# Raw gate banks, earlier squares and paired chains at the four joints of a hybrid encoder layer

## The chip, the cores and the metric

The kernel runs on one core of one Trainium2 chip. The metric is the device time of one execution in microseconds, the median of three runs. TensorE is PE in the profile, VectorE DVE, ScalarE ACT, GpSimd POOL; SyncE (SP) issues the DMAs.

## The reference

One layer over 1024 tokens of width 1024, all in float32. Every sub-layer has its own norm, and the two SwiGLUs enter with a factor of one half:

```
def rmsnorm(x, g):
    return x * lax.rsqrt(jnp.mean(x * x, axis=-1, keepdims=True) + EPS) * g

def swiglu(h, w_gu, w_down):
    gate, up = jnp.split(h @ w_gu, 2, axis=-1)
    return (jax.nn.silu(gate) * up) @ w_down

x = x + 0.5 * swiglu(rmsnorm(x, ffn1_norm), ffn1_w_gu, ffn1_w_down)
h = rmsnorm(x, mix_norm); proj = h @ w_in        # HGRN2 group, stick-breaking group (q, k, v)
x = x + concat(hgrn2(...), stick_breaking(...)) @ w_out
x = x + memory_cross_attention(rmsnorm(x, mem_q_norm), rmsnorm(mem, mem_kv_norm), ...)
x = x + 0.5 * swiglu(rmsnorm(x, ffn2_norm), ffn2_w_gu, ffn2_w_down)
return rmsnorm(x, final_norm)
```

Widths: 1024 (model), 2816 (SwiGLU), 256 memory tokens in 4 heads, 8 stick-breaking heads of 64.

## The kernel before

Activations lie transposed: 8 chunks of 128 channels (c) by two halves of 512 tokens (hf). An fp32 product is made of three fp32r matmuls (`mm3`): high by high, low by high, high by low part. A chain of 8 such steps, 24 matmuls of 512 columns, fills one PSUM bank. The high part of a factor is an ACT copy, the low part a DVE subtraction (`factor`, `split`, `lift_chunk`).

The norm is applied after the matmul: with h = x·g as factor, a projection is multiplied by 1/rms of its token. For that, squares of the chunks (ACT) are summed over chunks (POOL, `arrive`), summed over partitions by one-column matmuls against `ones` (`sums_of_squares`), turned into 1/rms by twelve small DVE operations (`rsqrt`), and spread over 128 partitions by four 128x128 matmuls against `ident`, which ACT copies to the tile `rs` (`spread`).

A SwiGLU works on products of 512x512 blocks in a Strassen-Winograd scheme: seven products (A11, S1, S2, A12, S3, S4, A22) of sums of activations (tiles T1 to T4, made by `sums_12`, `sums_3`, `sums_4` on POOL, ACT and DVE) and sums of weights (`r` from HBM, `S` on POOL, `f` high on ACT and low on DVE). `pairs` weaves two such jobs; `pairs.start(n)` issues the weight work of the first products ahead, `pairs.run` the rest, `pairs.defer(n, step)` puts a step behind the n-th product. Ahead of the products stand plain chains for the first 256 columns: gates (banks X, Y), ups (Z, Z, X, Y). In the first SwiGLU the gate banks are still in PSUM when 1/rms comes. `between` scales them with `rs` (DVE), applies Silu (ACT), multiplies by `rs` again (POOL), so that `s` = silu(gate) × 1/rms, and the ups are multiplied in.

In the second SwiGLU (`stored=True`) the gates were made inside cross-attention (`gate_steps`), copied to HBM (`gd`) and loaded back. Its `rs` needs the last chunk that cross-attention delivers. The last two gate chains run one after the other, with the sums for the second token half between them.

At the end of the first SwiGLU the last chunks arrive, `inv_rms_both` (in `to_mixers`) makes the mixers' 1/rms, and `sb_proj(0, r)` runs chains for q and k of both halves in the two `acc` banks, with `spread_both` before step 7, then the values. Scores (`z_steps`, bank z) and their products of 1 - sigmoid (tile `om`: ACT, POOL mask, DVE scan) follow.

Engines run their queues in order. A planner (Tile) orders what the program issues by priority and dependences, and `tc.issue_after` pins an instruction behind another.

## Time and profile before

| | us |
|---|---|
| median of 3 runs | 2268.94 |
| lowest, highest run | 2266.56, 2270.53 |
| profiled execution | 2266.65 |
| its span | 2264.9 |
| PE busy in the span | 2192.8 |
| DVE, ACT, POOL busy | 1661.7, 1003.8, 730.4 |
| mean granted clock of PE | 0.993 |

The span is from the first to the last instruction of the profiled execution; that execution's own time has 1.75 us around it. PE is busy for 97% of the span, but "busy" counts a matmul at half clock as well as one at full clock. The idle rest is 72.1 us. The list of PE's waits names the larger pieces of it, and windows of the span give the granted clock of each stretch.

### The profile page before, as it was taken

The page shows a single profiled execution, that of the slowest core. Times are in us where ns is not written, and L with a number is a line of the kernel's source. Part 1 is how long each engine was busy: PE and PEld are TensorE (multiplying, and loading weights), DVE is VectorE, ACT ScalarE, POOL GpSimd, SP SyncE. Part 2 cuts the span into 40 slices and gives each one's busy share as a digit, 9 for nine tenths or more (in the row PEclk, how much of TensorE's full clock was granted, in tenths as well). Part 3 has the DMA queues.
Part 4 walks back from the last instruction along what each step waited for, and adds up shares of the span by engine and source line. Part 5 has one row for each costly group of instructions (what it writes and reads, how often), then busy time and mean ns, then how long its engine had stood idle before and what let it go on. Part 6 is the DMA issues. An engine that isn't in the chain of part 4 may idle for free.

```text
span 2264.9 us, 30630 instructions
## 1 busy us (share of the span) xinstructions
PE 2192.8 (97%) x10952; PEld 1837.0 (81%) x10952; DVE 1661.7 (73%) x2732; ACT 1003.8 (44%) x1905; POOL 730.4 (32%) x700
## 2 busy tenths in 40 slices
PE   8999999999999999999989999999999999999997
PEld 6888888878778787888879888887778888887876
DVE  7877777768986869778787455667786767685896
ACT  7544434443355536454464243224543444444334
POOL 3563535334541102020131020001355343443553
PEclk9999999999999999999999999999999999999999
DMA  8334434766721001100115311111342333377552
GB/s 298 130 128 135 142 128 147 254 213 215 244 96 38 23 25 29 38 29 19 38 54 161 93 48 47 47 38 47 125 145 93 131 120 126 124 259 233 180 175 75
DMA packets 220568, 265.75 MB, mean 117 GB/s; under 512 B 13440, under 2 KB 144512, under 8 KB 220416
## 3 DMA queue, kind: packets, MB, share of 16 engines
q1 hardware_dynamic: 220416, 263.80, 35.5%
q8 instruction: 86, 1.41, 0.3%
q14 instruction: 66, 0.54, 0.1%
HBM read 187.47 MB, written 76.28 MB: 116 GB/s over the span
## 4 chain that ended last, share of the span: by engine, by line
PE 79%; DVE 12%; ACT 3%; issue 2%; DMA 2%; POOL 1%; SPq 0%; POOLq 0%; DVEq 0%; ACTq 0%
PE X L82 26%; PE Y L82 13%; PE Z L82 6%; PE acc L127 4%; PE acc L129 4%; PE acc L128 4%; PE q L128 2%; PE q L127 2%; PE q L129 2%; DVE E L82 1%; DVE om L1143 1%; PE wo L129 1%; PE wo L127 1%; PE wo L128 1%; PE dn L127 1%
## 5 line engine op out<-in xcount | busy, mean ns | idle before, releaser
L82 PE MATMUL X<-T,f 128*128 128x512 f32 x1464 | 345.2, 391 | 3.7 <-ACT e L82 3.3
L82 PEld LDWEIGHTS X<-T,f 128*128 128x128 f32 x1464 | 275.4, 188 | 62.4 <-ACT e L82 3.8
L82 PE MATMUL X<-hh,f 128*128 128x512 f32 x975 | 311.9, 390 | 1.3 <-DVE E L82 0.9
L82 ACT ACTIVATE f<-S 128x512 fp32r<-128x512 f32 (+2 forms) x256 | 155.6, 609 | 269.6 <-POOL S L82 256.4
L82 DVE TENSOR_TENSOR f<-S,f 128x512 fp32r<-128x512 f32 (+2 forms) x256 | 226.3, 896 | 26.1 <-ACT f L82 25.4
L82 PEld LDWEIGHTS X<-hh,f 128*128 128x128 f32 x975 | 183.0, 188 | 41.9 <-issue 2.4
L82 POOL TENSOR_TENSOR E<-E,rs 128x512 f32<-128x512 f32 x104 | 170.4, 1638 | 126.4 <-DVE E L82 109.1
L82 DVE TENSOR_TENSOR f<-r,f 128x512 fp32r<-128x512 f32 (+2 forms) x192 | 201.3, 1065 | 0.0
L82 PE MATMUL X<-hl,f 128*128 128x512 f32 x488 | 190.9, 391 | 3.6 <-DVE hl L82 3.6
L82 POOL TENSOR_TENSOR S<-r,r 128x512 f32<-128x512 f32 (+2 forms) x64 | 94.1, 1470 | 307.9 <-DMA r<-in_ffn_w_down_dram 93.9
L82 PE MATMUL Y<-T,f 128*128 128x512 f32 x732 | 176.4, 389 | 0.0
L82 PE MATMUL Y<-hh,f 128*128 128x512 f32 x488 | 160.7, 389 | 0.0
L82 PEld LDWEIGHTS Y<-T,f 128*128 128x128 f32 x732 | 137.4, 188 | 28.7
L82 PE MATMUL Z<-hh,f 128*128 128x512 f32 x488 | 160.6, 389 | 0.0
L127 PE MATMUL acc<-hh,wh 128*128 128x512 f32 (+1 forms) x384 | 151.6, 395 | 0.0
L128 PE MATMUL acc<-hl,wh 128*128 128x512 f32 (+1 forms) x384 | 145.6, 379 | 2.5 <-DMA hl<-msl 2.5
L129 PE MATMUL acc<-hh,wl 128*128 128x512 f32 (+1 forms) x384 | 146.5, 382 | 0.0
L82 DVE TENSOR_TENSOR E<-X,E 128x512 f32<-128x512 f32 x100 | 68.7, 687 | 101.6 <-PE X L82 100.9
L82 POOL TENSOR_TENSOR S<-S,r 128x512 f32<-128x512 f32 (+2 forms) x64 | 83.2, 1300 | 180.7 <-DVE f L82 146.5
L1140 POOL TENSOR_SCALAR_AFFINE_SELECT om<-om 128x128 f32<-128x128 f32 x64 | 27.2, 425 | 340.3 <-ACT om L1135 340.0
L82 ACT ACTIVATE E<-X 128x512 f32<-128x512 f32 x102 | 60.5, 593 | 165.2 <-PE X L82 165.2
L107 ACT ACTIVATE wh<-wraw 128x512 fp32r<-128x512 f32 (+1 forms) x128 | 79.2, 654 | 90.5 <-PE acc L128 29.3
(455 smaller groups left out, 5433.7 us busy)
## 6 DMA issues: line engine op xcount, KB each, us to landing
r<-in_ffn_w_gu_dram SPq DMA_DIRECT2D x86, 512.0 KB, 3.8
r<-in_ffn_w_down_dram SPq DMA_DIRECT2D x32, 512.0 KB, 4.5
wraw<-in_w_in_dram SPq DMA_DIRECT2D x20, 512.0 KB, 3.6
wraw<-in_mem_w_kv_dram SPq DMA_DIRECT2D x16, 512.0 KB, 3.6
x<-in_x_cols_dram SPq DMA_DIRECT2D x16, 256.0 KB, 5.4
T<-in_x_dram SPq DMA_DIRECT2D x8, 512.0 KB, 6.1
fx<-x SPq DMA_DIRECT2D x16, 256.0 KB, 5.2
sg<-fx SPq DMA_DIRECT2D x16, 256.0 KB, 4.1
```

Of the source, the lines that this page charges most:

```text
L82: done = getattr(self.eng, name)(*args, **kw)
L107: nc.scalar.activation(hi[:, part], src[:, part], AF.Copy)
L127: nc.tensor.matmul(ps, lh, rh, start=start, stop=False)
L128: nc.tensor.matmul(ps, lh, rl, start=False, stop=False)
L129: last_mm[0] = nc.tensor.matmul(ps, ll, rh, start=False, stop=stop).ins
L1140: nc.gpsimd.affine_select(out=a[:, dg], in_=a[:, dg], compare_op=ALU.is_gt, fill=fill, base=0, pattern=[[-sign, P]], channel_multiplier=sign)
L1143: nc.vector.tensor_tensor_scan(run, run, run, 1.0 if carry is None else carry, op0=ALU.mult, op1=ALU.bypass)
```

## The change

It works at four places.

**First SwiGLU, start.** The four gate banks are copied raw to SBUF by DVE ahead of `rsqrt`; the spread of each half moves from the second Z chain into the X chain of the second half's ups and to its end; scaling follows there, from SBUF. `sums_4` of chunks 2 and 3 goes behind the first product, ahead of `sums_3`; the weight work of products 1 and 2 goes ahead of the scaling.

**First SwiGLU, end.** Squares of the first half are kept in tiles of their own (`rs0`, with chunk 7's apart in `rs1`); those of chunk 6, second half, are added by POOL. The two q chains of pair 0 stop after six of eight steps, the sums of squares stand between them and the rest, and the k chains use the z banks. The scaling of q comes after the fourth k step.

**Cross-attention.** The last head's softmax weights are scaled by ACT. The first half's sums are made when chunk 1 of the second half arrives, spread at chunk 3, and both first-half gates are finished there: DVE multiplies, ACT Silu, POOL multiplies. The last two gate chains alternate step by step in banks q and pt.

**Second SwiGLU, start.** Only the second half's gates are scaled there, after `pairs.start` of products 1 and 2; one spread stands before the second Z chain.

```diff
-    def arrive(c, hf, g0, sqp, acc, lift=True, apart=False):
+    def arrive(c, hf, g0, sqp, acc, lift=True, apart=False, kept=False):
         first = hf not in acc
-        sq = (accp if hf else sqp).tile([P, H], F32, name="sqa") if first else sqp.tile([P, H], F32, name="sq", bufs=2)
+        if kept and (first or apart):
+            sq = accp.tile([P, H], F32, name="sqa") if first and hf else rsp.tile([P, H], F32, name="rs1" if apart else "rs0")
+        else:
+            sq = (accp if hf else sqp).tile([P, H], F32, name="sqa") if first else sqp.tile([P, H], F32, name="sq", bufs=2)
...
+            def spread_one(hf):
+                with tc.issue_after(last_mm[0]):
+                    rs[hf] = spread(ys[hf], psn, "nm", rsp, f"rs{hf}")
...
-            flow([sums_4(j) for j in range(4 if stored else 2)], 2)
+            ups = [[plain(up, m, 0, "Z", 0, (lambda: spread_one(1)) if stored and m else None) for m in range(2)], None]
             if not stored:
+                for hf in range(2):
+                    for m in range(2):
+                        dve.tensor_copy(s[hf][m], gps[hf][m])
+                early, late = s
                 y = rsqrt(ys, 8, 1.0 / D, "h", eng=dve)
                 ys = [y[:, 0:4], y[:, 4:8]]
-            ups = [[plain(up, 0, 0, u_banks[0])], None]
-            ups[0].append(plain(up, 1, 0, u_banks[1], 0 if stored else 6, lambda: spread_both(rs, ys, psn, "nm", last_mm[0])))
...
+            for n in (1, 2):
+                pairs.start(n)
             if stored:
-                factors_first()
...
+                flow([scaled(s[1][m], late[m], 1) for m in range(2)], 1)
+            flow([sums_4(j) for j in (0, 1)], 2)
+            if not stored:
+                ups[1] = [plain(up, m, 1, "XY"[m], 4 * (1 - m), lambda: spread_one(m)) for m in range(2)]
+                flow([scaled(s[hf][m], (early, late)[hf][m], hf) for hf in range(2) for m in range(2)], 1)
+            else:
+                ups[1] = [plain(up, m, 1, "XY"[m]) for m in range(2)]
+            pairs.start(3)
...
+            pairs.defer(1, lambda: flow([sums_4(j) for j in (2, 3)], 2))
             pairs.defer(1, x_away)
...
-        ys[:] = inv_rms_both(acc, psn, "nm")
+        mix_acc.update(acc)
...
+    def sb_proj_first(r):
+
+        units = {n: load_cols(mw, w_in, [c0]) for n, c0 in (("q", 2048), ("k", 2560))}
+        banks = {("q", hf): psa.tile([P, H], F32, name="acc") for hf in range(2)}
+        banks.update({("k", hf): psz.tile([P, H], F32, name="z") for hf in range(2)})
+        chains = {at: proj_steps(ps, units[at[0]], hT[at[1]], EVEN_FIRST) for at, ps in banks.items()}
+        for n, hf, steps in (("q", 0, 6), ("q", 1, 6), ("q", 0, 2), ("q", 1, 2), ("k", 0, 8), ("k", 1, 8)):
+            for i in range(steps):
+                next(chains[n, hf])
+                if (n, hf, steps, i) == ("q", 1, 6, 2):
+                    ys[:] = inv_rms_both(mix_acc, pst, "tr")
+                if (n, hf, i) == ("k", 0, 3):
+                    spread_both(rs, ys, pst, "tr", last_mm[0])
+                    for h in range(2):
+                        sb_evict("q", h, banks["q", h], r)
+                yield
+            if n == "k":
+                sb_evict("k", hf, banks[n, hf], r)
+        yield from sb_values(0, r)
...
-            if (d, hf) == (7, 0):
+            if (d, hf) == (1, 1):
                 ys2.append(inv_rms(0, acc2, psp, "pt"))
+            if (d, hf) == (3, 1):
+                rs[0] = spread(ys2[0], psp, "pt", rsp, "rs0")
...
-            ps = psq.tile([P, H], F32, name="q")
+            ps = psp.tile([P, H], F32, name="pt") if (m, hf) == (1, 1) else psq.tile([P, H], F32, name="q")
...
-            nc.scalar.activation(t, ps, AF.Copy)
+            if hf == 0:
+                nc.vector.tensor_tensor(t, ps, rs[0], op=ALU.mult)
+                nc.scalar.activation(t, t, AF.Silu)
+                nc.gpsimd.tensor_tensor(t, t, rs[0], op=ALU.mult)
+            elif m == 1:
+                nc.vector.tensor_copy(t, ps)
+            else:
+                nc.scalar.activation(t, ps, AF.Copy)
...
-                nc.vector.tensor_scalar(pr[t], pr[t], sm, None, op0=ALU.mult)
+                if (n, hf) == (3, 1):
+                    nc.scalar.activation(pr[t], pr[t], AF.Copy, scale=sm)
+                else:
+                    nc.vector.tensor_scalar(pr[t], pr[t], sm, None, op0=ALU.mult)
...
-        for _ in gate_steps(0, 1):
-            pass
-        with tc.issue_after(last_mm[0]):
-            ys2.append(inv_rms(1, acc2, psp, "pt"))
-        for _ in gate_steps(1, 1):
-            pass
+        last = [gate_steps(m, 1) for m in range(2)]
+        for i in range(DC + 1):
+            for steps in last:
+                next(steps, None)
+            if i == DC - 1:
+                with tc.issue_after(last_mm[0]):
+                    ys2.append(inv_rms(1, acc2, psp, "pt"))
```

In the rows of the order below, `hh` and `hl` are a chunk's high and low part with token half and tile number, `f` a weight factor, `nm` the bank of a spread or of sums, `y8h` the eight columns of 1/rms.

PE before, in the second Z chain of the first SwiGLU's ups:

```order
L128 MATMUL Z<-hl_0_210,f 128x512
L129 MATMUL Z<-hh_0_209,f 128x512
L218 MATMUL nm<-ident,y8h 128x128 x4
L127 MATMUL Z<-hh_0_219,f 128x512
L128 MATMUL Z<-hl_0_220,f 128x512
L129 MATMUL Z<-hh_0_219,f 128x512
L127 MATMUL Z<-hh_0_229,f 128x512
L218 MATMUL nm<-ident,y8h 128x128 x4
L128 MATMUL Z<-hl_0_230,f 128x512
```

PE after, inside the X chain that follows the two Z chains:

```order
L127 MATMUL X<-hh_1_271,f 128x512
L128 MATMUL X<-hl_1_272,f 128x512
L129 MATMUL X<-hh_1_271,f 128x512
L221 MATMUL nm<-ident,y8h 128x128 x4
L127 MATMUL X<-hh_1_281,f 128x512
L128 MATMUL X<-hl_1_282,f 128x512
L129 MATMUL X<-hh_1_281,f 128x512
L127 MATMUL X<-hh_1_291,f 128x512
```

The two spreads left the end of the second Z chain; the first now stands 18 matmuls further down, the second another 12 below it, at the end of the X chain.

PE before, behind the last product of the first SwiGLU (`wh`, `wl`: the weight's parts; `sqa`, `sg`: squares):

```order
L82 MATMUL X<-T_5455,f 128x512 x3
L198 MATMUL nm<-ones,sqa 128x1
L127 MATMUL acc<-hh_0_5607,wh 128x512
L128 MATMUL acc<-hl_0_5608,wh 128x512
L129 MATMUL acc<-hh_0_5607,wl 128x512
L127 MATMUL acc<-hh_0_5738,wh 128x512
L128 MATMUL acc<-hl_0_5739,wh 128x512
L198 MATMUL nm<-ones,sg 128x1
L198 MATMUL nm<-ones,sqa 128x1
```

PE after, at the same place: the last eight matmuls ahead of the sums, all of the second half's q chain (`rs_5470` holds the first half's squares, `rs_5909` chunk 7's):

```order
L127 MATMUL acc<-hh_1_5722,wh 128x512
L128 MATMUL acc<-hl_1_5723,wh 128x512
L129 MATMUL acc<-hh_1_5722,wl 128x512
L127 MATMUL acc<-hh_1_5863,wh 128x512
L128 MATMUL acc<-hl_1_5864,wh 128x512
L129 MATMUL acc<-hh_1_5863,wl 128x512
L127 MATMUL acc<-hh_1_5866,wh 128x512
L128 MATMUL acc<-hl_1_5867,wh 128x512
L201 MATMUL tr<-ones,rs_5909 128x1
L201 MATMUL tr<-ones,rs_5470 128x1
```

Before, five chain matmuls, all of one half, stood between the first sum and the rest of sixteen; now eight of each half stand between the first sum and the rest of twelve.

POOL before, at the start of the second SwiGLU's products (`r` weight blocks, `S` their sums, `sg` the gates):

```order
L82 TENSOR_TENSOR S<-r_15750,r_15752 128x512
L82 TENSOR_TENSOR S<-S,r_15750 128x512
L82 TENSOR_TENSOR S<-r_15750 128x512
L82 TENSOR_TENSOR sg<-sg,rs_15717 128x512 x2
L82 TENSOR_TENSOR sg<-sg,rs_15724 128x512 x2
L82 TENSOR_TENSOR S<-r_15763,r_15765 128x512
L82 TENSOR_TENSOR S<-r_15752,S 128x512
```

POOL after:

```order
L82 TENSOR_TENSOR S<-r_15735,r_15737 128x512
L82 TENSOR_TENSOR S<-S,r_15735 128x512
L82 TENSOR_TENSOR S<-r_15735 128x512
L82 TENSOR_TENSOR sg<-sg,rs_15709 128x512 x2
L82 TENSOR_TENSOR S<-r_15748,r_15750 128x512
L82 TENSOR_TENSOR S<-r_15737,S 128x512
```

Two of the four gate multiplications, those by the first half's `rs`, are no longer between the first three weight sums and the next ones.

## Rows read from the trace of the kernel before

**Rows 1.** The head of the profile's page: the span, and the first line of its part 1, busy time, share of the span and instructions of each engine.

```profile
span 2264.9 us, 30630 instructions
...
PE 2192.8 (97%) x10952; PEld 1837.0 (81%) x10952; DVE 1661.7 (73%) x2732; ACT 1003.8 (44%) x1905; POOL 730.4 (32%) x700
```

**Rows 2.** The list of what TensorE (PE) waited for over the whole span: operation and line that waited, releaser, us in total, times, longest.

```profile
PE nm L218 <- DVE y8h L82: 3.9, 1, 3.9
PE X L82 <- ACT e L82: 3.3, 1, 3.3
PE nm L198 <- ACT sg L173: 2.8, 1, 2.8
PE pt L1595 <- DVE p L1586: 1.4, 1, 1.4
PE Z L127 <- ACT f L422: 1.2, 1, 1.2
PE pt L198 <- POOL fh L177: 1.1, 1, 1.1
...
PE q L128 <- DVE hl L191: 0.8, 1, 0.8
```

**Rows 3.** PE's timeline at the start of the first SwiGLU: start in us, duration, engine, line, operation, out<-in, tile and operand shape, count, and in brackets the idle time before it with its releaser.

```profile
40.39 0.39 PE L129 MATMUL Z<-hh,f 128*128 128x512 f32 x1
44.71 1.92 PE L218 MATMUL nm<-ident,y8h 128*128 128x128 f32 x8 [3.93 <-DVE y8h L82]
...
48.13 1.12 PE L218 MATMUL nm<-ident,y8h 128*128 128x128 f32 x8
...
49.56 0.39 PE L127 MATMUL X<-hh,f 128*128 128x512 f32 x1
...
60.44 0.39 PE L79 MATMUL X<-hh,f 128*128 128x512 f32 x1
...
71.32 0.39 PE L82 MATMUL X<-hh,f 128*128 128x512 f32 x1
```

**Rows 4.** The same stretch by windows, PE alone: the window, its length, PE busy time with instructions, the granted clock as a share of full, the DMA share and GB/s.

```profile
40.00:45.00 5.00, 1.07 (x6) 0.98 1.05 356
45.00:50.00 5.00, 5.00 (x24) 0.67 1.05 406
```

**Rows 5.** The timelines of the other engines in that stretch, columns as in group 3: five pieces of VectorE (DVE), one of GpSimd (POOL).

```profile
38.43 1.41 DVE L82 SCALAR_TENSOR_TENSOR e<-x,G,e 128x512 f32<-128x512 f32 x2
...
42.18 0.17 DVE L82 TENSOR_SCALAR ms<-ss 128x8 f32<-128x8 f32 x1
...
44.39 0.17 DVE L82 SCALAR_TENSOR_TENSOR y8h<-u,y8h 128x8 f32<-128x8 f32 x1
...
51.12 2.96 DVE L82 SCALAR_TENSOR_TENSOR t<-x,G,t 128x512 f32<-128x512 f32 x2
...
71.66 0.68 DVE L82 TENSOR_TENSOR f<-S,f 128x512 fp32r<-128x512 f32 x1
...
49.28 5.96 POOL L82 TENSOR_TENSOR sg<-sg,rs 128x512 f32<-128x512 f32 x4 [27.71 <-ACT sg L82]
```

**Rows 6.** PE's timeline at the end of the first SwiGLU and the start of the mixers, columns as in group 3.

```profile
660.83 0.40 PE L128 MATMUL acc<-hl,wh 128*128 128x512 f32 x1
664.00 0.38 PE L198 MATMUL nm<-ones,sg 128*128 128x1 f32 x2 [2.77 <-ACT sg L173]
664.24 0.36 PE L198 MATMUL nm<-ones,sqa 128*128 128x1 f32 x2
...
668.55 0.77 PE L129 MATMUL acc<-hh,wl 128*128 128x512 f32 x1
...
676.84 1.95 PE L218 MATMUL tr<-ident,y8h 128*128 128x128 f32 x16
```

**Rows 7.** That stretch by windows, PE alone, columns as in group 4.

```profile
665.00:670.00 5.00, 5.00 (x27) 0.61 0.02 3
670.00:675.00 5.00, 5.00 (x17) 0.71 0.73 203
```

**Rows 8.** ACT and DVE there, columns as in group 3.

```profile
663.33 0.62 ACT L173 ACTIVATE sg<-E 128x512 f32<-128x512 f32 x1
...
662.89 3.38 DVE L82 SCALAR_TENSOR_TENSOR hl<-E,G,hh 128x512 fp32r<-128x512 f32 x5
...
668.81 0.68 DVE L108 TENSOR_TENSOR wl<-wraw,wh 128x512 fp32r<-128x512 f32 x1
```

**Rows 9.** The start of the first pair of stick-breaking heads: PE's first score matmul (columns as in group 3); then the window of the pair's value chains with the instructions on the tile om alone, and two windows of its attention with everything (window, length, busy time with instructions of PE, PEld, DVE, ACT, POOL, granted clock, DMA share, GB/s).

```profile
693.17 0.28 PE L1130 MATMUL z<-sk,sq 128*128 128x256 f32 x1
...
694.00:717.00 23.00, 0.00 (x0) 0.00 (x0) 3.37 (x6) 1.15 (x3) 1.16 (x3) 1.00 0.09 25
...
730.00:750.00 20.00, 18.49 (x106) 15.16 (x105) 18.44 (x32) 14.03 (x28) 3.90 (x13) 1.00 0.04 12
750.00:770.00 20.00, 18.28 (x106) 15.16 (x105) 18.96 (x44) 11.99 (x26) 4.21 (x10) 1.00 0.05 16
```

**Rows 10.** The start of the second SwiGLU: POOL's and PE's timelines, columns as in group 3, and one window of PE, columns as in group 4.

```profile
1637.78 5.81 POOL L82 TENSOR_TENSOR sg<-sg,rs 128x512 f32<-128x512 f32 x4 [1.89 <-ACT sg L82]
...
1646.01 0.80 PE L82 MATMUL X<-T,f 128*128 128x512 f32 x1 [3.34 <-ACT e L82]
...
1645.00:1650.00 5.00, 3.99 (x11) 0.66 0.14 52
```

More of the change, by code (lines that the diff above doesn't have):

```diff
@@ L692, in plain @@
                     for k in range(2):
-                        if at == 2 * j + k:
+                        if between and at == 2 * j + k:
                             between()
@@ L851, in read @@
                                         "A22": ("X", 1, 0, True)}[fk]
-                    if fk == "A11" and ends and not plain_last and "sq" not in pools:
-                        pools["mps"].close()
-                        pools["sq"] = pool(st, "fsq", 1)
+                    if fk == "A11" and ends and not plain_last and "mps" in pools:
+                        pools.pop("mps").close()
                     if plain_last and ends:
@@ L1047, in place, with sb_evict @@
         return t if t < 4 else 7 - t
+    def sb_evict(n, hf, ps, r):
+        nc.vector.tensor_tensor(ps, ps, rs[hf], op=ALU.mult)
+        pair = [sbk.tile([P, H], F32R, name=f"s{n}{hf}{e}") for e in range(2)]
+        for e, t in enumerate(pair):
+            own, other = (slice(64 * i, 64 * i + 64) for i in (e, 1 - e))
+            nc.scalar.activation(t[own, :], ps[own, :], AF.Copy)
+            if n == "q":
+                nc.vector.tensor_tensor(t[other, :], ps[own, :], t[own, :].bitcast(F32), op=ALU.subtract)
+            else:
+                nc.scalar.activation(t[other, :], ps[own, :], AF.Copy)
+        if n == "k":
+            low = [(accp.tile([P, H], F32R, name="sqa") if hf and e else
+                    sbp.tile([P, H], F32R, name=f"skl{hf}{e}")) for e in range(2)]
+            for e, t in enumerate(pair):
+                own = slice(64 * e, 64 * e + 64)
+                for rows in (own, slice(64 - 64 * e, 128 - 64 * e)):
+                    nc.vector.tensor_tensor(low[e][rows, :], ps[own, :], t[own, :].bitcast(F32), op=ALU.subtract)
+            r["kl", hf] = low
+        r[n, hf] = pair
+    def sb_proj_first(r):
[13 more added lines that the diff above has]
+                yield
+            if n == "k":
+                sb_evict("k", hf, banks[n, hf], r)
+        yield from sb_values(0, r)
     def sb_proj(p, r):
@@ L1054, in sb_proj, with sb_values @@
                 yield from proj_steps(ps, unit, hT[hf], EVEN_FIRST)
-                nc.vector.tensor_tensor(ps, ps, rs[hf], op=ALU.mult)
-                pair = [sbk.tile([P, H], F32R, name=f"s{n}{hf}{e}") for e in range(2)]
-                for e, t in enumerate(pair):
-                    own, other = (slice(64 * i, 64 * i + 64) for i in (e, 1 - e))
-                    nc.scalar.activation(t[own, :], ps[own, :], AF.Copy)
-                    if n == "q":
-                        nc.vector.tensor_tensor(t[other, :], ps[own, :], t[own, :].bitcast(F32), op=ALU.subtract)
-                    else:
-                        nc.scalar.activation(t[other, :], ps[own, :], AF.Copy)
-                if n == "k":
-                    low = [(accp.tile([P, H], F32R, name="sqa") if hf and e else
-                            sbp.tile([P, H], F32R, name=f"skl{hf}{e}")) for e in range(2)]
-                    for e, t in enumerate(pair):
-                        own = slice(64 * e, 64 * e + 64)
-                        for rows in (own, slice(64 - 64 * e, 128 - 64 * e)):
-                            nc.vector.tensor_tensor(low[e][rows, :], ps[own, :], t[own, :].bitcast(F32), op=ALU.subtract)
-                    r["kl", hf] = low
-                r[n, hf] = pair
+                sb_evict(n, hf, ps, r)
+        yield from sb_values(p, r)
+    def sb_values(p, r):
         units = [load_cols(mw, w_in, [3072 + P * p, 1024 + P * p], k0=k0, kn=4) for k0 in (0, 4)]
@@ L1509, in hybrid_layer @@
         psd = pool(st, "psdc", 2, PSUM)
+        psq = pool(st, "psq", 2, PSUM)
         cs = st.enter_context(ExitStack())
```

32 lines of the change are left out of this document (8 added, 24 removed).

## The prediction

> **What bounds the kernel now.** The head of the page comes first: PE is busy for 2192.8 of 2264.9 us [rows 1], so the other engines matter only where PE waits for them or where PE runs slowly. Next comes the list of PE's waits [rows 2]. The change is aimed at seven of its entries: 3.9 at the first SwiGLU's spread, 2.8 at the mixers' sums of squares, 1.4, 1.1, 0.8 and 1.2 in and behind cross-attention, 3.3 at a product of the second SwiGLU. The reader should see that these are single waits at joints, each on a short chain of other engines. Then the timelines of PE at the joints [rows 3, 6, 10], to see what stands behind each wait, and the windows over them [rows 4, 7, 10], because a wait costs twice where the granted clock falls behind it: three long waits are each followed by windows at 0.61 to 0.71. A share between 0.5 and 1 is a window that is partly at 1.2 GHz and partly at 2.4. What the clock takes from a 5 us window is (1 - share) x 5. At full clock, 48 matmuls of two chains run from 49.56 to 60.44 [rows 3], 0.227 us each.
>
> **Place A, start of the first SwiGLU.** Removed: the wait of 3.93 [rows 3] and (1 - 0.67) x 5 = 1.65 in the window behind it [rows 4], together 5.6. Added on DVE ahead of the rsqrt: four copies from PSUM. No such copy is in these rows; the nearest are the two operations of 1.41 at 38.43, 0.7 each, and at the other end the two of 2.96, 1.5 each [rows 5]. I take 0.7, because POOL does nothing at 38 us (its first piece there starts at 49.28 after 27.71 idle). They take the place of work that held the rsqrt until 42.18, so 1/rms is ready at 38.43 + 2.8 + (44.39 + 0.17 - 42.18) = 43.6 [rows 5]. PE reaches the old place at 40.39 + 0.23 = 40.62 [rows 3] and now has 6 matmuls of Z and 12 of X ahead of the spread: 40.62 + 18 x 0.227 = 44.7. So 1.1 us cover the wait; at 1.5 a copy, 2.1 of it come back. PE's chains then end at 40.62 + 54 x 0.227 + two spreads of 0.9 (half of 1.95, [rows 6]) = 54.7, where it is 60.44 now.
>
> Two things can hand some of that back. First, ACT copies the spread to rs behind copies for weight sums that now stand ahead; the bank nm is one, so the second spread waits if rs is late. Its cover is the 12 matmuls between, 2.7 us. Four copies at 0.62 (a piece of ACT of that width, [rows 8]) are 2.5 and fit; with two DVE operations of 0.7 between them they are 3.9 and 1.2 shows. I take nothing and keep 1.2 as the other end. Second, sums_4 of chunks 2 and 3, four DVE operations, now stands ahead of sums_3. Today sums_3 is done at 71.66 [rows 5] and product S3 starts at 71.32 + 12 x 0.227 = 74.04 [rows 3]: 2.4 in hand. In the new order DVE's last gate multiplication cannot start before 54.7; with it and behind it stand three f, four operations of sums_4 and eight of sums_3, sixteen of 0.7 [rows 5], ending at 65.9, while S3 falls to 54.7 + 13.6 = 68.3. The same 2.4 are left, unless POOL works beside DVE, where two operations took 2.96 instead of 1.41 [rows 5], 0.8 more for each. Three or four such meetings use the slack up. I charge 0.6, with 0 and 2.1 as ends. **A gives 5.6 - 0.6 = 5.0, from 2.3 to 5.7.**
>
> Ahead of the first products the four gate multiplications change from one operand in PSUM to two in SBUF. DVE's pairs of 1.41 and 2.96 [rows 5] differ by whether POOL worked. The Trainium skill, "SBUF — State Buffer", section "SBUF: two separate sides", says that a VectorE operation with two SBUF inputs and a GpSimd operation reading SBUF lock a shared port pair against each other for a whole instruction. By it the four would take up to 5.9 where mine are taken at 2.8, and the slack at S3 could turn to -0.7, so that the sum would be 16.5 and not the 17.2 below. The trace agrees in kind: 2.96 against 1.41.
>
> **Place B, end of the first SwiGLU.** Removed: the wait of 2.77 [rows 6]; the clock behind it, (0.39 + 0.29) x 5 = 3.4 [rows 7]; four of sixteen sums at 0.22 to 0.24 (a pair starts at 664.00, the next at 664.24, [rows 6]), 0.9. Together 7.1. What is late next: today's fifth chain matmul starts at 660.83 [rows 6], and with eleven more PE is busy to 660.83 + 12 x 0.227 = 663.55; the last square ends at 663.33 + 0.62 = 663.95 [rows 8], a wait of 0.4. Eleven sums end at 666.5. The chain's next weight half must be split by DVE, which does it right behind the hl work that ends at 662.89 + 3.38 = 666.27, in 0.68 [rows 8]: 666.95, another 0.5. That leaves 6.2.
>
> The rest is paid later. The first score now stands ahead of the value chains, at 693.17, and DVE does 3.37 of scans and products for three tiles beside the value chains [rows 9]. With k in the z banks, all scores follow the values, so this lands in the attention, where DVE is busy 18.44 and 18.96 of 20 and PE idles 1.5 and 1.7 [rows 9]. Either DVE's free 2.6 take it (0) or PE waits for all (3.4), or also a first latency of about 1.1 a tile (4.6). I charge 1.1, a third, since both engines have slack there. **B gives 5.1, from 1.6 to 6.2.**
>
> **Place C, cross-attention and start of the second SwiGLU.** Removed: the wait of 3.34 and (1 - 0.66) x 5 = 1.7 of clock [rows 2, 10]; 1.4 + 1.1 + 0.8 + 1.2 of the joints [rows 2]. Together 9.5. What stays: the 1.4 is DVE's scaling of softmax weights; ACT does it now, but the reciprocal remains in DVE's queue behind a chunk's low part: 0.7 stay. The sums of the first half stand later, where their square is long done: 0. The last gate chains alternate and reach chunk 7 seven steps later: 0. Of the 1.2, ACT's copies start sooner, but DVE must copy a gate and alternates the low parts with the rsqrt: 0.7 stay. At the product, POOL had four gate multiplications in 5.81 ahead of the weight sum [rows 10]; two are gone, 2.9 of 3.34, so 0.4 stay. The slack at S3 is charged 0.6 as in A. The ends: of the 1.4 and the 1.2 nothing or all stays, at the product 0.4 or 0.8, at S3 0 or 2.1. The moved gate work, two multiplications each on DVE and POOL, two Silu and a table load on ACT, lies beside the output projection and costs nothing while POOL and ACT have gaps there; without that cover the first half's squares come late by some 2 us, and two rows of [rows 2] return. **C gives 7.1, from 4.0 to 9.1.** A gain beyond the waits and the clock removed is excluded at all three places: the matmuls are the same but for the four sums.
>
> **Sum.** 5.0 + 5.1 + 7.1 = 17.2 from the profiled execution's own 2266.65: 2249.45. That execution lies 2.29 below the median of the runs, 2268.94, so the median of the changed kernel is put at **2251.7**. All gains at their upper end, 21.0, against the profiled time without that offset: 2245.65. All at the lower end, 7.9, with it: 2261.0.
>
> **The rivals.** (1) *DVE is late at S3 in both SwiGLUs.* The deferred sums meet POOL throughout: 3.5 us beyond the slack's use (four operations at 1.5 less the 2.4 in hand), with a clock drop of 1.65 behind, 5.1 a place, of which 0.6 is counted: 2251.7 + 9.0 = 2260.7. For it: DVE is the busiest engine after PE, and the slack is 2.4. Against: half of the gate work leaves C. 0.13. (2) *The stall of A moves.* ACT stands in its queue at a weight sum that waits for POOL and for a landing, rs is late, the second spread waits and the clock falls: A gives nothing, 2256.7. For: four ACT copies now stand ahead of rs. Against: the cover of 2.7. 0.12. (3) *Slower.* Pair 0 of the attention runs without lead: each of its 24 score tiles (8 in the first half, 16 in the second) shows its own chain to PE. A tile's part on DVE alone is 3.37 / 3 = 1.1; 24 of them are 27, and 2251.7 + 27 = 2278.7. It decides from 0.9 a tile, 21.7 in all, where the gain of 17.2 and 0.2% are gone. For: DVE at 92 and 95% there. Against: six buffers let the scores run ahead again, and only three tiles lose their lead. 0.04. (4) *It doesn't do what it says.* Weight sums now stand ahead of the gates on POOL; if their blocks land late, gates and products wait as long as today in A and C, 12.1 in all, and B's 5.1 goes into the attention: 2268.9. 0.05. (5) *No new wait shows:* 2245.6 to 2249. 0.12.
>
> **How the numbers follow.** The forecast has 0.54. The range from 2245.6 to 2261.0 takes in the forecast, (1), (2) and (5). Leaving out no more than 2 in 10 would allow less, but the bounds of the sum reach that far. A change of 0.2%, 4.5 us, is about what a measurement of this kernel can tell from none: faster by more 0.91, within it 0.05, slower 0.04.
>
> **What the profile after would show.** A: no wait of PE on y8h, the first product near 54.7, windows from 40 to 50 at full clock; wrong if PE waits at a spread or at S3. B: short waits near 663.5 and 666.5, the last k matmul near 686.8; more idle of PE in pair 0 would show the price. C: no wait on e of the third product, and the joints' entries gone from the list. Wrong altogether: a wait of PE over 3 us that the list does not have now, with a window at a lower clock behind it.

## The result, and the profile after

The changed kernel takes **2255.15 us** (median of 4 runs, 2252.07 to 2257.70) against 2269.49 for the kernel before on the same chip (4 runs, 2266.56 to 2270.53): a ratio of 0.9938, 95% interval 0.9921 to 0.9956. It is faster by 0.6%, within the range forecast; 2251.7 was the forecast. Its profiled execution took 2256.96. Run again beside the first experiments it took 2252.38 (5 runs, 2251.40 to 2255.70), ratio 0.9943 (0.9927 to 0.9959).

The head of the page after, answering to [rows 1], and then the entries of PE's list of waits that stand where those of [rows 2] stood:

```profile
span 2255.2 us, 30618 instructions
...
PE 2189.7 (97%) x10944; PEld 1834.2 (81%) x10944; DVE 1669.5 (74%) x2733; ACT 1004.2 (45%) x1906; POOL 732.6 (32%) x701
```

```profile
PE X L82 <- ACT E L82: 4.0, 3, 2.4
...
PE acc L127 <- ACT wh L107: 1.5, 1, 1.5
...
PE nm L221 <- ACT rs L224: 1.1, 1, 1.1
```

All seven waits that the prediction named are gone from the list. Three came: the copies E out of the bank that product S3 writes, in both SwiGLUs; the second half of a weight (`wh`) at the mixers' start; and `rs` at the second spread, which needs the bank that ACT copies to `rs`. In PE's timeline (start, duration, operation, in brackets the idle time before it and its releaser), at the places of [rows 3], [rows 6] and [rows 10]:

```profile
45.52 1.05 PE L221 MATMUL nm<-ident,y8h 128*128 128x128 f32 x8
50.43 1.16 PE L221 MATMUL nm<-ident,y8h 128*128 128x128 f32 x8 [1.10 <-ACT rs L224]
56.91 0.39 PE L79 MATMUL X<-hh,f 128*128 128x512 f32 x1
72.02 0.50 PE L82 MATMUL X<-hh,f 128*128 128x512 f32 x1 [1.34 <-ACT E L82]
...
662.16 0.50 PE L127 MATMUL acc<-hh,wh 128*128 128x512 f32 x1 [1.51 <-ACT wh L107]
664.56 1.62 PE L201 MATMUL tr<-ones,rs 128*128 128x1 f32 x14
...
1643.33 0.50 PE L82 MATMUL X<-hh,f 128*128 128x512 f32 x1 [2.44 <-ACT E L82]
```

The windows over them, PE alone (length, busy time, granted clock, DMA share, GB/s), for [rows 4], [rows 7] and [rows 10]:

```profile
45.00:50.00 5.00, 4.32 (x23) 1.00 1.06 406
...
70.00:75.00 5.00, 3.66 (x16) 1.00 0.17 52
...
665.00:670.00 5.00, 5.00 (x29) 0.81 0.43 115
670.00:675.00 5.00, 5.00 (x20) 0.85 0.39 109
...
1640.00:1645.00 5.00, 2.56 (x10) 0.93 0.16 29
1645.00:1650.00 5.00, 5.00 (x17) 0.72 0.20 77
```

What the reader should see: the clock behind the first SwiGLU's spread stays at 1.00 where it was 0.67, and PE no longer waits for 1/rms itself, only 1.10 for its bank; but S3 waits in both SwiGLUs, and the clock still falls behind the weight and behind the second S3.

Where the time came from is read by laying the two PE timelines over each other: for the same matmul, its start before less its start after is the lead of the changed kernel, and what a stretch adds to the lead is its gain. The last column has other executions of the study in which that stretch was as in the changed kernel. The kernel before has one trace, and all leads are against it.

| stretch (us of the kernel before) | forecast | after | again | others |
|---|---|---|---|---|
| start and A, to 170 | 5.0 | 1.9 | 2.6 | 1.6 to 2.8 |
| rest of the first SwiGLU, to 650 | 0 | -1.1 | -0.8 | -0.4 to 0 |
| B with pair 0, to 811 | 5.1 | 2.2 | 2.2 | 0.2 to 3.8 |
| rest of mixers, cross-attention to 1545 | 0 | 1.1 | 3.5 | -1.8 to 6.2 |
| C, to 1760 | 7.1 | 6.5 | 8.2 | 6.6 to 8.2 |
| rest, to the end | 0 | -1.0 | -0.8 | -1.5 to 0.3 |
| sum | 17.2 | 9.6 | 15.0 | |

The first row has the start in it, where nothing was changed and where the executions lie between 2.6 behind and 0.4 ahead of the kernel before at 36 us; counted from there A gave 2.7 and 2.5, and 2.8 to 4.3 in the others. So A and B gave about half in the two traces of the changed kernel, C what was forecast, and a stretch that the change doesn't touch moved the sum by up to 8 between executions, more than any miss. The engines at A, answering to [rows 5]: DVE, then ACT, then POOL.

```profile
42.66 1.15 DVE L82 SCALAR_TENSOR_TENSOR u<-u,ms 128x8 f32<-128x8 f32 x1
45.70 3.47 DVE L82 SCALAR_TENSOR_TENSOR e<-x,G,e 128x512 f32<-128x512 f32 x2
50.53 1.29 DVE L82 TENSOR_TENSOR sg<-sg,rs 128x512 f32<-128x512 f32 x2
53.36 2.60 DVE L82 TENSOR_TENSOR sg<-sg,rs 128x512 f32<-128x512 f32 x2 [1.54 <-ACT rs L224]
57.17 1.74 DVE L82 TENSOR_TENSOR f<-S,f 128x512 fp32r<-128x512 f32 x1 [1.22 <-ACT f L82]
60.63 0.68 DVE L82 TENSOR_TENSOR sg<-sg,Y 128x512 f32<-128x512 f32 x1
63.03 1.41 DVE L82 SCALAR_TENSOR_TENSOR t<-x,G,t 128x512 f32<-128x512 f32 x2
70.35 1.36 DVE L82 TENSOR_TENSOR hl<-t,hh 128x512 fp32r<-128x512 f32 x2
...
49.26 0.63 ACT L82 ACTIVATE T<-e 128x512 fp32r<-128x512 f32 x1 [1.07 <-DVE e L82]
49.80 0.58 ACT L224 ACTIVATE rs<-nm 128x512 f32<-128x512 f32 x1
50.39 1.28 ACT L82 ACT_TABLE_LOAD   x1
71.38 0.59 ACT L82 ACTIVATE E<-X 128x512 f32<-128x512 f32 x1
...
42.47 1.31 POOL L82 TENSOR_TENSOR S<-r,r 128x512 f32<-128x512 f32 x1 [21.10 <-DVE y8h L82]
...
52.40 5.97 POOL L82 TENSOR_TENSOR sg<-sg,rs 128x512 f32<-128x512 f32 x4 [3.78 <-ACT sg L82]
```

`rs` is copied at 49.80, though its bank was written by 46.57: in ACT's queue the copies T of `sums_4` stand ahead, and they wait for two DVE operations that took 3.47 beside POOL. Behind it DVE scales the gates; the second pair waits 1.54 for the second `rs` and takes 2.60 while POOL multiplies (until 58.37), where the first pair took 1.29. ACT's Silu and a factor copy follow, then DVE's low part of that factor, 1.74 beside POOL, until 58.91. Only then come the four multiplications by the ups, the last at 60.63, though PE began its first product at 56.91. DVE's sums run from 63.03 to 71.7, and E, behind their copies on ACT, ends at 71.97; S3 starts at 72.02.

ACT at the end of the first SwiGLU, answering to [rows 8] (`sg` squares, `hh` lifts of the last chunks):

```profile
660.34 0.63 ACT L176 ACTIVATE sg<-E 128x512 f32<-128x512 f32 x1 [0.85 <-DVE E L82]
660.88 0.71 ACT L82 ACTIVATE hh<-E,G 128x512 fp32r<-128x512 f32 x1
661.50 1.14 ACT L107 ACTIVATE wh<-wraw 128x512 fp32r<-128x512 f32 x2
```

The copy of the weight's second half, for which PE waits until 662.16, stands behind a square for which ACT itself waits 0.85, and behind a lift.

### The profile page after: what moved, and what is told of

Same layout as the page of the kernel before. It is cut to its first block, busy times and chain, and to the rows that moved or that the text cites. A ratio compares the mean times of both kernels' runs of the same rounds, so it can differ in the third digit from the quotient of the medians.

```text
span 2255.2 us, 30618 instructions
## 1 busy us (share of the span) xinstructions
PE 2189.7 (97%) x10944; PEld 1834.2 (81%) x10944; DVE 1669.5 (74%) x2733; ACT 1004.2 (45%) x1906; POOL 732.6 (32%) x701
## 3 DMA queue, kind: packets, MB, share of 16 engines
q8 instruction: 86, 1.41, 0.3%
## 4 chain that ended last, share of the span: by engine, by line
PE 78%; DVE 12%; ACT 3%; issue 2%; DMA 2%; POOL 1%; SPq 0%; POOLq 0%; DVEq 0%; ACTq 0%
PE X L82 26%; PE Y L82 13%; PE Z L82 6%; PE acc L127 4%; PE acc L129 4%; PE acc L128 4%; PE q L127 2%; PE q L128 2%; PE q L129 2%; DVE om L1169 2%; PE dn L127 1%; PE dn L129 1%; PE dn L128 1%; PE wo L129 1%; PE wo L127 1%
## 5 line engine op out<-in xcount | busy, mean ns | idle before, releaser
L82 DVE TENSOR_TENSOR f<-S,f 128x512 fp32r<-128x512 f32 (+2 forms) x256 | 231.4, 916 | 25.4 <-ACT f L82 24.6
L127 PE MATMUL acc<-hh,wh 128*128 128x512 f32 (+1 forms) x368 | 144.7, 393 | 1.5 <-ACT wh L107 1.5
L128 PE MATMUL acc<-hl,wh 128*128 128x512 f32 (+1 forms) x368 | 139.0, 378 | 2.6 <-DMA hl<-msl 2.6
L129 PE MATMUL acc<-hh,wl 128*128 128x512 f32 (+1 forms) x368 | 139.2, 379 | 0.0
```

The source lines that it names most:

```text
L82: done = getattr(self.eng, name)(*args, **kw)
L127: nc.tensor.matmul(ps, lh, rh, start=start, stop=False)
L128: nc.tensor.matmul(ps, lh, rl, start=False, stop=False)
L129: last_mm[0] = nc.tensor.matmul(ps, ll, rh, start=False, stop=stop).ins
```

## The experiments

Every median below has 5 or 6 runs, beside at least 9 of the kernel before on the same chip, whose medians were 2265.96 to 2267.78. The interval of a ratio is some 3 to 4 us to each side of the median, and every one overlaps that of the changed kernel run again (0.9927 to 0.9959): the medians alone set none of these edits apart from it. What an edit is worth is read in the traces, one execution each.

**The changed kernel again**, unedited.

> The changed kernel once more, unedited, as the yardstick of the others. All theories: 2252 to 2258 us; at the first S3 products PE waits about 1.3 and 2.4 us for the copies of bank X (ACT), as in its first trace. If the differences of 0.8 us at the start, 1.1 us in the first SwiGLU's loop and 1.3 us at the tail come from one execution to the next, they are other here; if they belong to the change, they stay.

Measured: 2252.38. Its trace has the same waits; the lead at the end is 15.0 instead of 9.6. Of the 5.4 between two executions of one program, 2.4 arise between 811 and 1545, 1.7 at C, where the clock did not fall behind S3, and 0.7 at the start. The loss in the rest of the first SwiGLU is 0.8 here and 0 to 0.4 in other executions of the same code, so it comes with the execution and not with the change.

**The fourth sums ahead of the third product's weights.**

```diff
+            flow([sums_4(j) for j in (2, 3)], 2)
             pairs.start(3)
...
-            pairs.defer(1, lambda: flow([sums_4(j) for j in (2, 3)], 2))
```

> The sums_4 of chunks 2 and 3 stand ahead of the third product's start again, in both SwiGLUs, not behind the first product. Theory 'placed ahead of sums_3': the four DVE operations (2.8 us) then run while PE does its plain chains, DVE comes to sums_3 2.8 us earlier, both waits at S3 (1.3 and 2.4 us, with 1.8 us of clock behind the second) vanish: 5 us faster than the changed kernel. Rival 'DVE's sum': DVE has no free time before S3, the same operations only push the gate work back by 2.8 us, and S3 waits as before: within 1 us of the changed kernel, or slower if the third product now waits.

Measured: 2251.38, ratio 0.9935 (0.9921 to 0.9948). The waits of S3 shrink from 4.0 in the list to 0.8, and 2.7 on e appear at the third product (2 times, longest 2.0). The median is 1.0 below the changed kernel run again, where the first theory had 5. The wait moves with DVE's work: moving the sums ahead on DVE moves the wait to the product before.

**The fourth sums behind the third**, in both SwiGLUs, with PSUM banks as scratch of `sums_3`.

```diff
-                u = tp.tile([P, H], F32, name="t")
+                u = (psn, psx)[j % 2].tile([P, H], F32, name=("nm", "aux")[j % 2])
...
                 flow([sums_3(j) for j in range(4)], 2)
+                flow([sums_4(j) for j in (2, 3)], 2)
...
-            pairs.defer(1, lambda: flow([sums_4(j) for j in (2, 3)], 2))
```

> The sums_4 of chunks 2 and 3 behind sums_3, whose scratch tiles go to the two idle PSUM banks nm and aux. Both theories of DVE's lateness: sums_3 is done 2.8 us earlier, the waits at S3 vanish, 5 us faster than the changed kernel in all. Rival 'the copies on ACT': the bank's copy waits for something other than sums_3, PE's waits on E stay at 1.3 and 2.4 us and nothing is gained. If T4 comes late instead, a wait on the last product of the first job appears.

Measured: 2251.40, ratio 0.9934 (0.9919 to 0.9949), 1.0 below instead of 5. In A the wait at S3 is gone; at the spread it is 1.85, and here the clock falls behind it (0.66 from 50 to 55, so 1.7 us). In C it stays at 2.08. ACT's timeline there says why:

```profile
1640.84 1.29 ACT L82 ACTIVATE T<-t 128x512 fp32r<-128x512 f32 x2 [1.42 <-DVE t L82]
1642.04 0.58 ACT L82 ACTIVATE E<-Y 128x512 f32<-128x512 f32 x1
1642.51 0.59 ACT L82 ACTIVATE E<-X 128x512 f32<-128x512 f32 x1
```

The third sums were complete at 1640.1 on DVE, yet E still ends at 1643.1, behind the copies T of sums that S3 does not need. In C it is ACT's order.

**The spread ahead of the fourth sums**, first SwiGLU.

```diff
-            flow([sums_4(j) for j in (0, 1)], 2)
+            if stored:
+                flow([sums_4(j) for j in (0, 1)], 2)
             if not stored:
...
+                flow([sums_4(j) for j in (0, 1)], 2)
             else:
```

> First SwiGLU only: sums_4 of chunks 0 and 1 behind the scaling of the gates, so that no T copy that waits for DVE stands ahead of rs on ACT. Theory 'rs is late': rs is copied at about 46.5 instead of 49.8, the wait of 1.1 us at the second spread goes, POOL's four gate multiplications start some 3 us earlier, and the 1.3 us at the first S3 go as well: 2 to 3 us faster than the changed kernel. Rival 'POOL and the landing': POOL's weight sums hold the gates, rs comes earlier but the gate multiplications do not end earlier by more than 1 us, S3 still waits: 1 us faster at most.

Measured: 2254.48, ratio 0.9950 (0.9935 to 0.9965), not faster, where the first theory had 2 to 3; S3 still waits, as its rival said. `rs` comes at 46.68, the spread no longer waits, the first product starts at 55.61 instead of 56.91, and S3 takes it all back:

```profile
72.64 0.50 PE L82 MATMUL X<-hh,f 128*128 128x512 f32 x1 [3.27 <-ACT E L82]
```

The late `rs` was real but not the only bound of A; DVE's work ahead of S3 was another.

**The fourth sums last**: chunks 1 to 3 out of both queues, chunk 0 behind the scaling.

```diff
+                u = (psn, psx)[j % 2].tile([P, H], F32, name=("nm", "aux")[j % 2])
...
                 flow([sums_3(j) for j in range(4)], 2)
+                rest = [sums_4(j) for j in range(1, 4)]
+                for c in rest:
+                    next(c)
+                pairs.defer(2, lambda: flow(rest, 2))
...
-            flow([sums_4(j) for j in (0, 1)], 2)
+            if stored:
+                flow([sums_4(0)], 1)
...
+                flow([sums_4(0)], 1)   # first SwiGLU, behind scaled
```

> In both SwiGLUs sums_4 of chunks 1 to 3 does its subtraction behind sums_3 and its split behind the third product, so that neither DVE nor ACT has it in the queue ahead of product S3 and ahead of the copies E of S1 and S2; sums_3 uses two PSUM banks as scratch. In the first SwiGLU chunk 0 stands behind the scaling too. Theory (DVE's work ahead of sums_3 in A, ACT's order in C): rs of the first spread by 47 us, first product near 55.6 instead of 56.9, no wait at S3 in either SwiGLU (1.34 and 2.44 in the changed kernel) and no clock drop behind it; 4 to 6 us below the changed kernel run again (2252.4), so 2246.5 to 2248.5. Rival (the next releaser, weight factors split by the same DVE or summed by POOL, is late by as much): a wait on e or f of 1 us or more at the third to fifth product instead, and a median within 1.5 us of 2252.4.

Measured: 2251.68, ratio 0.9937 (0.9922 to 0.9953), so by medians only 0.7 below the unedited kernel, less than expected. In the trace A does as expected: PE has no wait from 40 to 80 and the stretch from 36 to 100 gives 5.5, of which 1.1 is lost again before 120, with a wait of 0.73 on f at 114.44: 4.4 net. Counted in the same way the changed kernel has 2.7 and 2.5, and other executions with its code for A 2.8 to 4.3; the wait at S3, 1.15 to 1.35 in all of those, is gone here. In C, S3 still waits 1.06 and the product at 1652.85 another 1.06 on DVE's E: nothing is gained there over the unedited kernel's 6.5 to 8.2.

**Place B undone** (`sb_proj(0, r)`, `inv_rms_both` in `to_mixers`, sixteen sums).

```diff
-        for _ in sb_proj_first(r):
-            pass
+        for i, _ in enumerate(sb_proj(0, r)):
+            if i == 7:
+                spread_both(rs, ys, pst, "tr", last_mm[0])
...
-        mix_acc.update(acc)
+        ys[:] = inv_rms_both(acc, psn, "nm")
```

> Place B alone undone: q and k chains one after the other in the acc banks, sixteen sums of squares behind five chain matmuls, the spread before step 7, the first scores ahead of the values. By the ledger of the two traces (the lead of the changed kernel grows by 2.1 to 2.2 over this stretch, pair 0 of the attention included): median 2 to 2.5 us above the changed kernel, 2254.5 to 2255. By the prediction's sum: 5.1 above, 2257.5. In the trace: the wait of 2.8 on sg is back with a window near 0.61 behind it, the last k matmul is later by 4 to 4.5 relative to the last product, and the attention's first 25 us are shorter by 2.5 to 3.

Measured: 2256.13, ratio 0.9960 (0.9946 to 0.9974): 3.75 above the changed kernel, between the two expectations. Its trace has PE order as before, a wait of 3.19 on sg, and this clock, to be compared with 0.61 and 0.71 in [rows 7]:

```profile
660.00:665.00 5.00, 2.81 (x14) 0.62 0.28 105
665.00:670.00 5.00, 5.00 (x21) 0.50 0.01 3
670.00:675.00 5.00, 5.00 (x13) 0.52 0.71 205
```

That is (0.38 + 0.50 + 0.48) x 5 = 6.8 behind it, where the kernel before lost 3.4 in its profiled execution. For that the stretch from 650 to 811 is 3.2 longer here than in the kernel before. So B is worth 2.2 against the one execution of the old order and 5.5 against the other: much of what it is worth hangs on the clock behind the old wait.

**The second k chain in an acc bank.**

```diff
-        banks.update({("k", hf): psz.tile([P, H], F32, name="z") for hf in range(2)})
+        banks["k", 0] = psz.tile([P, H], F32, name="z")
...
+            if (n, hf) == ("k", 1):
+                banks[n, hf] = psa.tile([P, H], F32, name="acc")
+                chains[n, hf] = proj_steps(banks[n, hf], units[n], hT[hf], EVEN_FIRST)
```

> Place B: the second half's k chain goes into an acc bank again, so that the first half's scores have a free z bank ahead of the values. If the late scores are what gives back 2.7 us in pair 0 of the attention (windows 710 to 770), the first scores stand near 690, the attention's windows are as in the kernel before and the median is 2 to 3 us below 2252.4, unless the k chain now waits for the q bank by as much. If the loss is DVE's total work, which is the same in both, the first scores move and the median stays within 1 us of 2252.4.

Measured: 2256.93, ratio 0.9958 (0.9945 to 0.9971), 4.6 above the changed kernel run again, where both expectations had it level or below. Inconclusive on its question: the scores stayed behind the values, so the free bank was not what holds them there. The k chain waits 0.80 for q's eviction and the values 0.58, and place B gives 0.3 instead of 2.2.

**Place A undone**: for the first SwiGLU the lines of before, from `flow(sums_4)` to the gate multiplications.

```diff
+            if not stored:
+                flow([sums_4(j) for j in range(2)], 2)
+                y = rsqrt(ys, 8, 1.0 / D, "h", eng=dve)
+                ...
+                ups[0].append(plain(up, 1, 0, "Z", 6, lambda: spread_both(rs, ys, psn, "nm", last_mm[0])))
+            else:
...
-            pairs.defer(1, lambda: flow([sums_4(j) for j in (2, 3)], 2))
+            if stored:
+                pairs.defer(1, lambda: flow([sums_4(j) for j in (2, 3)], 2))
```

> Place A alone undone: gate banks stay in PSUM, both spreads in the second Z chain, sums_4 of chunks 2 and 3 behind the scaling. By the ledger of the traces (A kept 2.6 to 2.7 of its gain): median 2.5 to 3 us above the changed kernel, near 2255. By the prediction's sum: 5.0 above, 2257.4. If the gain of A were lost again later (the loop behind it lost 0.7 to 1.1): 1.5 to 2 above.

Measured: 2254.90, ratio 0.9952 (0.9936 to 0.9968), 2.5 above the changed kernel: near the ledger's value of A and half of the forecast's, but a median can't tell 2.5 from 5 here. In the trace the lead at 170 is -0.2: A's gain is gone.

**Scores ahead of the values.**

```diff
-        yield from sb_values(0, r)
...
+                heads = sb_attend(p, r, rest)
+                if p == 0:
+                    for _ in range(2):
+                        next(heads)
+                    for _ in sb_values(0, r):
+                        pass
-                interleave(sb_attend(p, r, rest), SB_STEPS, hg_proj(p, r), HG_PROJ_UNITS)
+                interleave(heads, SB_STEPS, hg_proj(p, r), HG_PROJ_UNITS)
```

> Place B: two score tiles of pair 0 are issued ahead of the value chains again, all else as in the changed kernel. If the late scores are what costs the attention 1.8 to 2.7 us in windows 710 to 770 (the second k chain in an acc bank did not move them, so that run could not tell), PE busy in 710 to 730 goes from 18.5 back to 19.3 of 20 and the lead at 760 grows by 1 to 2 us against the kernel before; median 2250.5 to 2251.5 against 2252.4. If DVE's total work of the pair decides, the lead at 760 is as in the changed kernel and the median too.

Measured: 2256.63, ratio 0.9950 (0.9935 to 0.9966), above both expectations. The first score starts at 687.8, before the values, and nothing is won. All engines (window, length, busy time of PE, PEld, DVE, ACT, POOL, clock, DMA share, GB/s), two windows of the changed kernel (which answer to [rows 9]) in the first block, the same two of this kernel in the second:

```profile
710.00:730.00 20.00, 18.48 (x101) 14.08 (x100) 16.19 (x29) 13.63 (x34) 7.74 (x22) 1.00 0.18 53
...
750.00:770.00 20.00, 18.27 (x107) 15.18 (x106) 19.35 (x39) 13.51 (x27) 4.11 (x11) 1.00 0.00 1
```

```profile
710.00:730.00 20.00, 17.61 (x98) 14.11 (x97) 18.21 (x31) 12.96 (x33) 8.27 (x20) 1.00 0.18 54
...
750.00:770.00 20.00, 17.31 (x92) 14.33 (x91) 18.60 (x32) 12.99 (x26) 3.39 (x10) 0.91 0.01 1
```

PE idles more, not less. The place of the scores is therefore not shown to be the price; the edit also shifts the fill by two steps, so what pair 0 pays for stays open.

**The first q weight copied whole.**

```diff
+            whole[0] = n == "q"      # split: one part instead of two
+            units[n] = load_cols(mw, w_in, [c0])
```

> Place B: ACT copies the first q weight in one piece of 1024 columns instead of two of 512 with the lifts of the last chunks between, so that the wait of 1.51 on wh has no cause. Theory: that wait is gone, PE waits next for a lift or a square of the last chunks, 0.2 to 0.9 in all, and the clock stays at 1.00 from 660 to 680; the step of place B in the ledger goes from 1.2 (with the clock drop) or 2.8 (without) to 3.4 to 4.3; median 1 to 3 us below 2252.4. Rival: the chunks' own high and low parts are late at the same point, and the wait only gets another name: 1.2 to 1.5 with the drop behind it, median as before.

Measured: 2251.70, ratio 0.9934 (0.9919 to 0.9949), within the interval of the changed kernel. The wait is gone, no other takes its place, and the clock stays:

```profile
660.00:665.00 5.00, 5.00 (x26) 1.00 0.30 110
665.00:670.00 5.00, 5.00 (x33) 1.00 0.38 106
```

From the first mixers' chain matmul to the last of k, PE takes 33.12 in the kernel before, 29.4 in the changed one (both executions), and 25.94 here. Up to 811 the ledger gives B 4.9, where the changed kernel has 2.2 and 3.4 to 4.3 were expected.

**The three edits together**: those of the last sums, of the scores and of the weight.

```diff
+                pairs.defer(2, lambda: flow(rest, 2))
...
+            whole[0] = n == "q"
...
+                    for _ in sb_values(0, r):
+                        pass
```

> The three edits together: fourth sums behind the third, scores ahead of the values, first q weight copied whole. If each waits at a place of its own the leads add: A 4.4 to 5.5 instead of 2.6, B 4.5 to 5.5 instead of 2 to 2.5 up to the end of pair 0, C as with the fourth sums last (7 to 7.5). Median 2246 to 2249, spread by the clock at the mixers' end. If the gains are taken back downstream as with the fourth sums last (median only 0.7 below): 2250 to 2251.

Measured: 2250.43, ratio 0.9934 (0.9920 to 0.9948). The lead at the value matmul that stands at 712 in the kernel before is 10.4; by 811 the rest of pair 0 takes 5.4 of it back, as the run with the scores ahead alone lost 4.8; the changed kernel itself gives back 3.3 from there. Up to 811 B gives 1.7, not 4.5 to 5.5: the gains do not add.

**The two that gained**: last sums in the first SwiGLU only, and the weight whole.

```diff
+                if not stored:
+                    rest = [sums_4(j) for j in range(1, 4)]
+                    ...
+                    pairs.defer(2, lambda: flow(rest, 2))
...
+            whole[0] = n == "q"
```

> The two edits that gained in the ledger, joined: in the first SwiGLU alone the fourth sums of chunks 1 to 3 behind the third and chunk 0 behind the scaling; the first q weight of the mixers copied whole; cross-attention, the second SwiGLU and the place of the scores as in the changed kernel. If places add: step of A 4.4 (5.5 less 1.1 given back by product 9), of B 4.5 to 4.9 through pair 0 with no clock drop at 665, of C 6.5 to 8.2; 3.5 to 5 us more lead than the changed kernel run again up to the mixers' end (8.5 to 9.5 against 4.0 at 811 of the kernel before). Median 2247 to 2250, against 2252.4, with a spread of up to 4 us from the mixers' end. If the waits only move: lead at 811 under 7 and a median above 2251.

Measured: **2248.22** (6 runs, 2246.17 to 2252.02), ratio 0.9925 (0.9909 to 0.9940): the lowest median of the study and 4.2 below the changed kernel's 2252.38 (by the ratios 4.1), though the two intervals still overlap. In the trace the places add: lead 4.3 at 170, 8.8 at 811, where the two traces of the changed kernel have 3.0 and 4.0.

## Why the prediction came out

**A: direction right, size wrong.** What it removes was right: 1/rms was ready at 44.0 (43.6 forecast), the first spread stands at 45.52 (44.7) without a wait, the clock stays. This execution was 0.8 late before anything that was changed. Both signs that the prediction set for A being wrong came: a wait at a spread and one at S3. The step that failed is "DVE's last gate multiplication cannot start before 54.7": it started at 60.63. It hangs on `rs`, late behind ACT's T copies, and on what follows it in turn on DVE and ACT, twice slowed beside POOL; not on PE, and not on POOL's four multiplications, which ended at 58.37 while DVE was still at a factor. The eleven microseconds from there to the end of the sums were right (60.63 to 71.7, 54.7 to 65.9), so the slack of 2.4 at S3 was gone: 1.34 instead of the 0.6 charged. The 1.2 at the spread, kept as an end and taken at nothing, came as 1.10. That DVE's and ACT's queues ahead of S3 were the bound is shown: the wait moves with the sums, an early `rs` alone returns as 3.27, and with both taken away no wait is left there, 4.4, near the 5.0.

A wait costs some 0.3 more than the list of waits says, where the traces allow a comparison: behind the 1.34 at S3 the lead falls by 1.64, and the 1.51 on `wh` makes the chains 1.81 longer where the clock stays (27.75 against 25.94). The forecast took the listed times.

The row of two DVE operations of 3.47 beside POOL, where the pairs at 63.03 took 1.41, agrees with the rule of the Trainium skill, "SBUF — State Buffer", section "SBUF: two separate sides", on two-input operations; so does the small operation at 42.66, which ends at 43.81, as POOL's sum from 42.47 does at 43.78, and takes 1.15 for it. Of the four gate multiplications by `rs` two met POOL: 3.9 in all, where the forecast took 2.8 and the sum by the rule of the Trainium skill up to 5.9. The other meetings, ahead of `rs` and at the factor, were in neither sum.

**B: the mechanism right, one releaser wrong.** The wait of 2.77 and four sums are gone. The forecast had two short waits, 0.4 on the last square and 0.5 on DVE's split of the next weight half. Neither shows. What came is the ACT copy of the first weight's second half, 1.51 at 660.65, queued behind a square and a lift, with 1.7 of clock behind it in the profiled execution. Without it the k chains take 25.94; the forecast, 686.8 - 659.82 = 27.0, is what the design gives once that copy is out of the way. The price in pair 0, charged 1.1, was 1.5: 3.7 less for the chains, but only 2.2 less up to 811. That is within its bounds; its cause is not settled.

**C: right in sum, by two errors that cancel.** 6.5 to 8.2 measured, 7.1 forecast. The 1.4 that were to stay at the joints, and the 0.4 at the product, are gone altogether; the wait at S3, charged 0.6, is 2.44, with (0.07 + 0.28) x 5 = 1.75 of clock. Its mechanism is the one of A with ACT's order at its end. By these terms C would be 5.3 in the first trace and 7.1 in the second; the further 1.1 to 1.2 fits the 0.3 by which the list understates each of the old waits, but was not traced one by one. C was not undone by itself.

**The sum.** The places of the changed kernel add up to 10.6 in the first profile and 13.0 in the second (A 1.9 and 2.6, B 2.2, C 6.5 and 8.2), not 17.2. That the medians still came 14.3 and 15.4 apart, 3.5 and 0.7 from the forecast, is in good part luck and no merit of the working. Their intervals, 10.0 to 17.9 and 9.3 to 16.6, hold the ledger's sums as well. And between 811 and 1545, where all engines run the same instructions in both kernels, the traces of the changed kernel gain another 1.1 and 3.5, because the profiled execution before lost 5.1 of clock there; of the 13 other traces 11 lost less, mostly 1.7 or 3.4. The forecast took that trace for typical there. What else the medians hold beyond the ledger stays open: that execution was itself 2.8 faster than the median of its four runs, and no slower one of the kernel before was traced.

**The rivals.** DVE late at S3 in both SwiGLUs was right in kind and too dear: 1.34 and 2.44 with one clock drop, against 5.1 a place. The stall of A moving to `rs` came at 1.10 without a drop, and with one in the run that had 1.85 there. The slower case did not come: pair 0 lost 1.5, not 27. Weight sums landing late did not show.

## What to carry to other kernels

When a step is moved ahead, list for each engine in whose queue it now stands everything behind it up to the next product, and count from the releaser that is really last; a DVE slack read from the old order is worth nothing if the gate of that queue hangs on another engine's. A copy that can be split into two pieces should not be, where other work falls between the pieces and PE needs the second soon after the first (here some 1.5 us). Before putting a difference of 2 us on an edit, lay the traces over each other and see whether it stands where the edit is.

## What the hardware showed that was not expected

The clock behind one and the same wait is not the same from one execution to the next. Behind the wait of 1.51 on wh (same place, same matmuls) the changed kernel lost 1.7 in its profile; with only the fourth sums moved, and the mixers' code as it was, it lost nothing:

```profile
661.82 0.50 PE L127 MATMUL acc<-hh,wh 128*128 128x512 f32 x1 [1.51 <-ACT wh L107]
...
665.00:670.00 5.00, 5.00 (x31) 1.00 0.40 111
670.00:675.00 5.00, 5.00 (x24) 1.00 0.49 138
```

From the first chain matmul to the last k it is 29.37 to 29.39 in four executions, 27.75 in three, and 31.37 in one, whose wait was 1.94, for the same instructions. At the mixers' end, where a chain waits for a transfer of `msl`, the changed kernel again and the run with the second k chain moved show the two ends (PE's timeline and windows of each):

```profile
1192.60 0.38 PE L128 MATMUL acc<-hl,wh 128*128 128x256 f32 x1 [1.97 <-DMA hl<-msl]
...
1195.00:1200.00 5.00, 5.00 (x44) 1.00 0.49 158
1200.00:1205.00 5.00, 4.97 (x43) 1.00 0.36 107
```

```profile
1194.55 0.58 PE L128 MATMUL acc<-hl,wh 128*128 128x256 f32 x1 [2.27 <-DMA hl<-msl]
...
1195.00:1200.00 5.00, 5.00 (x25) 0.50 0.79 262
1200.00:1205.00 5.00, 5.00 (x27) 0.54 0.00 1
```

Waits of 1.97 and 2.27 differ by 0.3; what follows them by (0.50 + 0.46) x 5 = 4.8. The runs of one kernel spread by 4 to 10, and no edit of the experiments moves the median by as much as 4.8. What decides between the levels was not tried.
